# Gathering the tokens of two experts at once with float32r products

## The chip, the cores and the metric

The kernel runs on one core of one Trainium2 chip. The metric is device time in microseconds (us): the median of several executions. TensorE is called PE in the profile, VectorE DVE, ScalarE ACT, GpSimd POOL, and SyncE, whose queue issues the loads of weights, SP. PEld is TensorE's loading of the stationary operand, which overlaps its products.

## The reference, cut to what matters

Two transformer blocks for 256 tokens of 1024 features, all in float32. The change is in the last layer's mixture of experts: 8 experts, each token goes to two of them.

```python
def moe_swiglu(xn, router_w, w_gate_up, w_down):
    xf = xn.reshape(-1, d_)                                  # 256 tokens x 1024
    logits = (xf @ router_w).astype(jnp.float32)
    top_v, top_i = lax.top_k(logits, TOP_K)                  # 2 of 8
    top_w = jax.nn.softmax(top_v, axis=-1)
    combine = jnp.sum(jax.nn.one_hot(top_i, N_EXPERTS, dtype=jnp.float32) * top_w[..., None], axis=1)
    out = jnp.zeros_like(xf)
    for e in range(N_EXPERTS):
        out = out + combine[:, e:e + 1] * swiglu(xf, w_gate_up[e], w_down[e])   # silu(g) * u, 3584 wide
    return out.reshape(b_, s_, d_)
```

## The kernel before

Every large product is exact to float32 by three float32r products: a matrix x is split into hi (its float32r rounding, copied by ACT) and lo = x - hi (subtracted by DVE), and hi·hi, lo·hi and hi·lo are added up in PSUM. Activations are split once, weights as they stream in.

**The stream of weights.** `load` (L223) brings 1 MB with one DMA into one of 7 raw buffers, or, where the plan allows it ("ANY", the experts' weights and the last output product), with four DMAs of 256 KB into four pages of a pool of 50 pages of [128, 512]. `fill` (L359) issues loads as long as fewer than `room[0]` = 7 raw and fewer than `room[1]` paged loads are held; `room[1]` follows a table by stage (`ROOM_MOE`, `ROOM_ROUTED`, `ROOM_FIRST`, `ROOM`). All go through SP's queue in order. Each load is two pieces; `look_ahead` (L375) splits a piece three pieces ahead of its use: one ACT copy and one DVE subtraction of 1024 columns from a raw buffer, two of 512 columns each from pages.

**The order of the work** is the order in which the program is written, on each engine. `unit` (L452) is one slot: first the PE part of the next stage of a side generator, then the products with one piece of weights (six products of 512 columns in an expert), then the split of a later piece, deferred work, and the rest of the side's stage (evacuations on ACT and DVE). A side advances by two `yield`s per unit; sides put in front go first.

**An expert** (`expert`, L1507) is 7 gate/up steps `j` of 8 units, each followed by silu, multiplication and a transposition of the result (`at`, L1519; split into `ah`, `al`), and two column halves `n` of 14 units of the down product (`y`, L1560 to L1562), whose result is scattered back to the tokens by products with `selT` (`po`, L1570).

**The gather** (`prepare`, L1469) runs as a side of the previous expert's down product, one per expert. `sel` [token, slot] holds ones where a token has that place in the expert's list. Products of the tokens `xn` (float32, stationary) with `sel` (float32, 128 columns) give the expert's tokens, transposed, as `xe` in PSUM (L1488); ACT and DVE split them into `xeh` and `xel`. `sel` is then transposed into `selT` (L1501, L1503, L1505). For expert 0 the generator starts in `moe` (L1441 to L1447) right after the routing: two stages, the split of one more piece of weights, two stages more, and the rest as an "urgent" side of the first units. PSUM tiles of all sides (`sp`) share four buffers.

Of the kernel before, what the change touches and what calls it, by code (L numbers as in the profile page):

```python
# [31 lines left out]
# columns of the packed parameters  # L32
# [19 lines left out]
# columns of the constants that depend on shapes alone  # L52
# [5 lines left out]
def shape_constants():  # L58
# [16 lines left out]
    # masks of the decay levels: [s, level, t]; the first is the diagonal  # L75
# [5 lines left out]
    # one-hot buckets over the distance, [bucket, set, y]  # L81
    oh = np.zeros((33, 2, 384), np.float32)
    y = np.arange(384)
    dist = y - 127                     # query - key
# [18 lines left out]
# buffers: loads of weights (8 KB), pages (2 KB), pieces split ahead; first products for the clock  # L103
RAW_BUFS, PAGE_BUFS, LOOK, WARM = 7, 50, 3, 10
RAW, ANY = 1, 2          # a load goes into a raw buffer, or also into four pages
# loads that may be in pages: from the last layer's merge on; with the experts' start, after the routing;
# while the first expert runs (seven steps, two column halves); later
ROOM_MERGE, ROOM_MOE, ROOM_ROUTED, ROOM_FIRST, ROOM = 4, 5, 8, (8, 8, 7, 7, 6, 6, 6, 6, 6), 6


class Norm:
    """rmsnorm of the stream: the split stream times the gains (x), the root per token (rs, and as columns col)."""
# [4 lines left out]
    def then(self, f):  # L117
        """f needs the root."""
        if self.ready:
            f()  # L120
        else:
            self.waiting.append(f)


class Net:
    """The two blocks. Engines run in the order in which instructions are written here: between the
    products with one piece of the weights ("unit") and the next go the split of a later piece,
    the evacuation of the last result and a stage of the attention-like parts ("side")."""
# [59 lines left out]
    def rsqrt(self, out, ms, tmp, scale=None):  # L188
        """out = (scale * ms + eps) ** -0.5: by exp and log, and by what it returns, a step of Newton's method."""
# [26 lines left out]
    def warm(self, n, x):  # L216
        """products that nothing reads, for TensorE's clock to stay up while it has to wait"""
        ps = self.sp("warm")
        for _ in range(n):
            self.nc.tensor.matmul(ps, self.ones_r, x.rearrange("p a b -> p (a b)"), start=True, stop=True)  # L220

# [14 lines left out]
    # plans yield RAW or ANY before each load, and for each piece its view (or views) and how many loads it is the last one of  # L236
# [9 lines left out]
    @staticmethod  # L246
    def halves(v):
        """the two pieces of a load with all columns"""
        if isinstance(v, list):
            n = len(v) // 2  # L250
            return v[:n], v[n:]
        n = v.shape[1] // 2
        return v[:, :n, :], v[:, n:, :]
# [105 lines left out]
    def fill(self):  # L359
        """loads as far ahead as there are buffers."""  # L360
# [14 lines left out]
    def look_ahead(self, far=LOOK):  # L375
        """the split of a later piece: ScalarE's part now, VectorE's with the next call."""
# [46 lines left out]
    def defer(self, f, n=1):  # L423
        """f is to run n slots later, when the other engines are through with what it needs."""
        self.later.append((n, f))
# [15 lines left out]
    def stage(self, width):  # L441
        """the first half (TensorE) of the next stage of the first sides; what remains of them."""
# [25 lines left out]
    def drain(self, width=2, gens=None):  # L468
        """runs sides alone until those in gens (or all) are through."""
# [19 lines left out]
    def chunk_t(self, x, evac, kb=8, width=1):  # L489
        """[P, 2, T] in PSUM: 256 columns of the weights, transposed, times x; then evac."""  # L490
# [7 lines left out]
    def chunk_late(self, x, evac, width=1):  # L498
        """as chunk_t with 8 blocks, the last two of the contraction taken after the others of both halves."""
# [17 lines left out]
    def scaled(self, out, ps, N):  # L517
        """out [P, 2, T] = a product in PSUM (one page or two halves) times the root of the norm."""
# [6 lines left out]
    def chunk_tok(self, x, evac, width=1):  # L525
        """two [P, 256] in PSUM: tokens on partitions, 256 columns of the weights; then evac."""
# [14 lines left out]
    def chunk_tok_pair(self, x, evacs, width=1):  # L541
        """two chunks, the second halves of the contraction after both first ones."""
# [17 lines left out]
    def norm_feed(self, N, c):  # L560
        """chunk c of the stream is complete."""
        self.gain(N, c)
        self.squares(N, c, self.nc.gpsimd)
        if c == 3:
            self.first.append(self.norm_root(N))

    def gain(self, N, c):
        """chunk c of the stream times the gains, split."""
# [8 lines left out]
    def squares(self, N, c, e):  # L577
        """squares of chunk c, added up: those of the first three by the engine e, VectorE the rest."""
# [34 lines left out]
    def first_chunk(self, N, xr, evac):  # L613
        """the norm of the stream as it comes in, with the first 256 columns of the weights two blocks at a time."""
# [7 lines left out]
        # products of ones, for TensorE's clock to be up when the first data are there  # L622
# [39 lines left out]
    def bias_tiles(self, which):  # L662
        """stages that make [P, 2, 256] pages, one per two heads: the bias of queries 128.. over all keys."""
# [40 lines left out]
    def block1(self):  # L704
# [5 lines left out]
        # lower bound: softmax over the two rows of gamma, first row  # L710
# [89 lines left out]
        gates = [self.pgv(2, T, nm="gl") for _ in range(8)]      # per 128 columns: [P, branch, T]  # L800
# [33 lines left out]
    def residual(self, x, kb, g):  # L834
        """the stream plus the product; the norm that follows, with gain g."""
# [39 lines left out]
    def head_scale(self, pages, width, N=None):  # L875
        """stages: rmsnorm of pages [P(t), 2 (tile), 256] over each width channels, in place, gains apart;
        with N, of the pages times the root of that norm."""
# [37 lines left out]
    def flip(self, x):  # L915
        """a page [P(t), 2 (tile), 256 (head, d)] as [P(d), 2 (head), T] in PSUM."""
# [6 lines left out]
    def flip_heads(self, xs, gs):  # L923
        """stages: pages with heads, [P(d), 2 (head), T], times gains."""
# [10 lines left out]
    def hgrn(self, qs, fs, ks, vs, sgs, mk, c, o):  # L935
        """two heads: q, f, k [P(dk), 2, T]; v [P(s), 2 (tile), 256 (head, dv)]."""
# [7 lines left out]
        for lev in range(8):  # L944
# [14 lines left out]
            else:  # L959
                # block length w -> 2w  # L960
# [37 lines left out]
    def soft(self, ps, bias):  # L998
        """logits of the first 128 queries over 128 keys and of the last over 256, in PSUM:
        exp(logits + bias - max), and the sums."""  # L1000
# [4 lines left out]
        for t in (1, 0):       # the part that is written last first  # L1005
# [8 lines left out]
    def pv(self, pts, v, tokens):  # L1014
        """stages: pts are probabilities per head, tokens on partitions; their products with v in PSUM,
        [P(t), 2 (tile), 256 (head, dv)] if tokens, or [P(dv), 2 (head), T]."""
# [97 lines left out]
    def layer_setup(self, l):  # L1114
        """stages; small loads and what they are made into."""
# [20 lines left out]
        lam = S["nlam"] = c.tile([P, 1], F32, name=f"nlam{l}")      # minus lambda  # L1136
# [54 lines left out]
    def pool(self, pa, S, l, ya):  # L1191
# [8 lines left out]
        shift(s0, pa, 1, al, slice(0, 2))      # windows of 2  # L1200
        shift(s1, s0, 2, al, slice(0, 2))      # 4
        yield 1
        yield 1
        shift(s0, s1, 4, al, slice(1, 2))      # 8, block 1
        shift(s1, s0, 8, hi, slice(1, 2))      # 16
# [13 lines left out]
        for b in (1, 0):       # the part that is written last first  # L1219
# [20 lines left out]
    def mixer(self, l, N, S):  # L1240
# [45 lines left out]
        # gates: per 128 columns two pages [P, 2 branches, T]: (attention, pool), (conv, sgu)  # L1286
# [43 lines left out]
    def moe(self, merged):  # L1330
        """the last layer's output product, tokens on partitions; routing; the experts."""
# [11 lines left out]
        def evac(c, ps):  # L1343
            cs = slice(256 * c, 256 * c + 256)
            y = self.xn[c] = self.pgv(2, 256, nm="xn")
# [4 lines left out]
            def stages():  # L1350
# [9 lines left out]
                self.copy(z, pt)  # L1360
                yield 1
# [4 lines left out]
                yield 1  # L1366
                sq = self.pg(nm="sq")
# [14 lines left out]
        # logits before the root of the norm, which the order doesn't depend on  # L1382
# [3 lines left out]
        # rank of each expert: how many are larger, or equal with a lower index  # L1386
# [15 lines left out]
        # positions of the tokens in their experts' lists  # L1402
# [10 lines left out]
        def weights():  # L1413
            """the root of the norm, the weights (softmax over the two chosen) and the longest list"""
# [30 lines left out]
        for _ in range(2):  # L1445
# [12 lines left out]
    def overflow(self):  # L1458
        """experts with more than 128 tokens: all experts again, for the tokens from the 129th on."""
# [9 lines left out]
    def prepare(self, e, pos, ready):  # L1469
        """stages: the tokens at positions 0..127 of pos in expert e's list, gathered by products."""  # L1470
        nc = self.nc
        mm = nc.tensor.matmul
        sel, sT = self.pg(nm="sel"), self.pg(dt=F32R, nm="selT")
        xe = []
        ready[e] = xe, sT
        yield 1
        for t in range(2):
            nc.vector.tensor_scalar(sel[:, t * P:t * P + P], self.c[:, C_IOTA:C_IOTA + P], pos[:, 8 * t + e:8 * t + e + 1], None, op0=OP.is_equal)
# [4 lines left out]
        for half in range(2):  # L1483
            ps = self.sp("xe")
            for k in range(4):
                kk = 4 * half + k
# [212 lines left out]
```

## Time and profile before

| | |
|---|---|
| time, median of 3 runs | 2203.89 us (2203.86 to 2204.39) |
| profiled execution: span from first to last instruction | 2202.1 us |
| the page's own time for that execution | none given beside its span; the median run is 1.8 us above the span |
| PE busy | 2180.7 us, 99% |
| DVE busy | 1794.9 us, 82% |
| ACT busy | 1438.9 us, 65% |
| moved by DMA | 559.89 MB, mean 254 GB/s over the span |

The experts take roughly the last 1000 us of the span. In the page, a line such as `L1488 PE MATMUL xe<-sel,xn` names the source line, the engine, the operation and its output and inputs; a float32 product shows as two records, a float32r product as one. A PE record's duration includes the pipeline, so records overlap; how far PE moves on per record is read from the chain of work that ended last, whose pieces lie end to end.

### The profile page before, as it was taken

The page shows a single profiled execution, that of the slowest core. Times are in us where ns is not written, and L with a number is a line of the kernel's source. Part 1 is how long each engine was busy: PE and PEld are TensorE (multiplying, and loading weights), DVE is VectorE, ACT ScalarE, POOL GpSimd, SP SyncE. Part 2 cuts the span into 40 slices and gives each one's busy share as a digit, 9 for nine tenths or more (in the row PEclk, how much of TensorE's full clock was granted, in tenths as well). Part 3 has the DMA queues.
Part 4 walks back from the last instruction along what each step waited for, and adds up shares of the span by engine and source line. Part 5 has one row for each costly group of instructions (what it writes and reads, how often), then busy time and mean ns, then how long its engine had stood idle before and what let it go on. Part 6 is the DMA issues. An engine that isn't in the chain of part 4 may idle for free.

```text
span 2202.1 us, 38213 instructions
## 1 busy us (share of the span) xinstructions
PE 2180.7 (99%) x14473; PEld 2000.6 (91%) x14473; DVE 1794.9 (82%) x2669; ACT 1438.9 (65%) x2159; POOL 82.3 (4%) x89
## 2 busy tenths in 40 slices
PE   9999999999999999999999999999999999999998
PEld 9999999999999999999998888888888888888886
DVE  7876766655787966557877999999999999999997
ACT  6447555444555554455555878888787878888785
POOL 0000000003000300020020000000000000000000
PEclk9999999999999999999999999999999999999999
DMA  9434466547553655574458999999999999999992
GB/s 331 148 128 141 135 193 191 186 160 221 184 167 106 222 192 172 171 222 156 156 175 299 344 325 365 350 361 373 341 368 340 371 348 363 345 368 368 333 372 79
DMA packets 386369, 559.89 MB, mean 254 GB/s; under 512 B 17482, under 2 KB 212058, under 8 KB 386176
## 3 DMA queue, kind: packets, MB, share of 16 engines
q1 hardware_dynamic: 383792, 552.04, 72.7%
q0 software_dynamic: 2240, 5.28, 0.8%
q8 instruction: 115, 1.88, 0.4%
q14 instruction: 78, 0.64, 0.1%
q10 hardware_dynamic: 144, 0.05, 0.0%
HBM read 556.23 MB, written 1.07 MB: 253 GB/s over the span
## 4 chain that ended last, share of the span: by engine, by line
PE 96%; DVE 3%; DMA 1%; issue 0%; SPq 0%; ACT 0%; DVEq 0%
PE g L485 13%; PE g L487 12%; PE g L486 12%; PE g L1542 9%; PE g L1540 9%; PE g L1541 9%; PE y L1560 5%; PE y L1562 5%; PE y L1561 5%; PE g L537 3%; PE g L539 3%; PE g L538 3%; DVE lo L400 1%; PE xe L1488 1%; PE lev L950 1%; PE at L1519 1%
## 5 line engine op out<-in xcount | busy, mean ns | idle before, releaser
L183 ACT ACTIVATE hi<-raw 128x512 fp32r<-128x512 f32 (+1 forms) x1382 | 1137.5, 849 | 589.2 <-PE g L486 283.0
L400 DVE TENSOR_TENSOR lo<-raw,hi 128x512 fp32r<-128x512 f32 (+1 forms) x1378 | 1289.7, 971 | 183.7 <-ACT hi L183 158.1
L485 PE MATMUL g<-nh,hi 128*128 128x256 f32 x1696 | 485.7, 286 | 0.7 <-ACT hi L183 0.7
L487 PE MATMUL g<-nh,lo 128*128 128x256 f32 x1696 | 480.1, 283 | 1.2 <-DVE lo L400 0.8
L486 PE MATMUL g<-nl,hi 128*128 128x256 f32 x1696 | 479.7, 283 | 0.0
L1540 PE MATMUL g<-hi,xeh 128*128 128x512 f32 x896 | 353.2, 394 | 0.0
L1542 PE MATMUL g<-lo,xeh 128*128 128x512 f32 x896 | 349.6, 390 | 0.0
L1541 PE MATMUL g<-hi,xel 128*128 128x512 f32 x896 | 349.0, 389 | 0.0
L485 PEld LDWEIGHTS g<-nh,hi 128*128 128x128 f32 x1696 | 325.1, 192 | 4.4 <-issue 1.8
L487 PEld LDWEIGHTS g<-nh,lo 128*128 128x128 f32 x1696 | 325.1, 192 | 1.8 <-DVE lo L400 1.0
L486 PEld LDWEIGHTS g<-nl,hi 128*128 128x128 f32 x1696 | 325.3, 192 | 0.2
L1542 PEld LDWEIGHTS g<-lo,xeh 128*128 128x128 f32 x896 | 168.2, 188 | 36.1 <-DVE lo L400 0.8
L1541 PEld LDWEIGHTS g<-hi,xel 128*128 128x128 f32 x896 | 168.4, 188 | 33.6
L1540 PEld LDWEIGHTS g<-hi,xeh 128*128 128x128 f32 x896 | 168.3, 188 | 33.2
L1560 PE MATMUL y<-hi,ah 128*128 128x512 f32 x448 | 177.0, 395 | 0.0
L1562 PE MATMUL y<-lo,ah 128*128 128x512 f32 x448 | 174.6, 390 | 0.0
L1561 PE MATMUL y<-hi,al 128*128 128x512 f32 x448 | 174.4, 389 | 0.0
L537 PE MATMUL g<-hi,nh 128*128 128x256 f32 x480 | 139.2, 290 | 0.0
L539 PE MATMUL g<-lo,nh 128*128 128x256 f32 x480 | 135.7, 283 | 0.0
L538 PE MATMUL g<-hi,nl 128*128 128x256 f32 x480 | 135.7, 283 | 0.0
L1562 PEld LDWEIGHTS y<-lo,ah 128*128 128x128 f32 x448 | 84.1, 188 | 17.7
L485 PE MATMUL g<-ah,hi 128*128 128x256 f32 x352 | 99.6, 283 | 0.0
(384 smaller groups left out, 2955.4 us busy)
## 6 DMA issues: line engine op xcount, KB each, us to landing
raw<-in_moe_w_gate_up_dram SPq DMA_DIRECT2D x122, 1024.0 KB, 5.8
raw<-in_moe_w_gate_up_dram SPq DMA_DIRECT2D x408, 256.0 KB, 6.0
raw<-in_w_in_dram SPq DMA_DIRECT2D x90, 1024.0 KB, 5.2
raw<-in_moe_w_down_dram SPq DMA_DIRECT2D x60, 1024.0 KB, 5.7
raw<-in_moe_w_down_dram SPq DMA_DIRECT2D x208, 256.0 KB, 6.3
raw<-in_ffn_w_gate_up_dram SPq DMA_DIRECT2D x22, 1024.0 KB, 5.2
raw<-in_w_ffn_gate_dram SPq DMA_DIRECT2D x11, 1024.0 KB, 5.4
raw<-in_w_ffn_up_dram SPq DMA_DIRECT2D x11, 1024.0 KB, 5.5
```

Source lines behind the costliest of these rows:

```text
L183: return self.nc.scalar.activation(out, in_, func, **kw)
L400: self.nc.vector.tensor_sub(l, x, h)
L485: mm(out, hi[:, k, :], xh, start=r + k == 0, stop=False)
L486: mm(out, hi[:, k, :], xl, start=False, stop=False)
L487: mm(out, lo[:, k, :], xh, start=False, stop=r + k == kb - 1)
L537: mm(ps[t], xh[:, s], hi[:, k, :], start=r + k == 0, stop=False)
L1540: mm(ps, xh, hi[:, k, :], start=first, stop=False)
L1541: mm(ps, xl, hi[:, k, :], start=False, stop=False)
L1542: mm(ps, xh, lo[:, k, :], start=False, stop=last)
L1560: mm(py, xh, hi[:, i, :], start=k == 0, stop=False)
L1561: mm(py, xl, hi[:, i, :], start=False, stop=False)
L1562: mm(py, xh, lo[:, i, :], start=False, stop=k == KE - 1)
```

## The change

- The normalised tokens `xn` (float32) are split as they are made, in the last output product's evacuation: `xh` on ACT, `xl` on DVE, four pages each in place of four pages of `xn`.
- `prepare` runs for the experts e and e+1 together, as a side of the down product of experts 1, 3 and 5, and before expert 0. `sel` is now one float32r page with 256 columns per token half: 128 for each of the two experts. Per 256 features (`c`), the parts `xh` and `xl` are multiplied with it in float32r, in two PSUM tiles; the gathered parts need no subtraction: ACT copies the one tile to `hi`, DVE the other to `lo`. Each of the four rounds is a stage of its own.
- The transposition to `selT` is done for each of the two experts, in a stage of its own each.
- Before expert 0, four stages (two rounds) in place of two (one half) stand ahead of the first unit.
- Fewer paged loads may be held: the table goes from 8 after the routing and 6 in the steady state down to 6 and 2.

```diff
-ROOM_MERGE, ROOM_MOE, ROOM_ROUTED, ROOM_FIRST, ROOM = 4, 5, 8, (8, 8, 7, 7, 6, 6, 6, 6, 6), 6
+ROOM_MERGE, ROOM_MOE, ROOM_ROUTED, ROOM_FIRST, ROOM = 4, 5, 6, (6, 6, 5, 5, 4, 4, 3, 2, 2), 2
...
-            y = self.xn[c] = self.pgv(2, 256, nm="xn")
+            y = self.pgv(2, 256, nm="xn")
+            xh, xl = self.xn[c] = [self.pgv(2, 256, dt=F32R, nm="xn" + s) for s in "hl"]
...
                 self.copy(z, pt)
+                self.copy(xh, y)
...
+                nc.vector.tensor_sub(xl, y, xh)
                 sq = self.pg(nm="sq")
...
         self.split_next(LOOK + 1)
-        for _ in range(2):
+        for _ in range(4):
             next(prep)
...
-        sel, sT = self.pg(nm="sel"), self.pg(dt=F32R, nm="selT")
+        page = self.pg(dt=F32R, nm="sel")
+        sel = page.rearrange("p (t e s) -> p t e s", t=2, e=2)
         xe = []
-        ready[e] = xe, sT
+        sTs = [self.pg(dt=F32R, nm="selT") for _ in range(2)]
+        for i in range(2):
+            ready[e + i] = xe, i, sTs[i]
...
-        for half in range(2):
-            ps = self.sp("xe")
-            for k in range(4):
-                kk = 4 * half + k
-                for t in range(2):
-                    mm(ps[:, k * P:k * P + P], self.xn[kk // 2][:, t, (kk % 2) * P:(kk % 2) * P + P], sel[:, t * P:t * P + P], start=t == 0, stop=t == 1)
-            yield 1
-            hi, lo = self.pg(dt=F32R, nm="xeh"), self.pg(dt=F32R, nm="xel")
-            self.copy(hi, ps)
-            sub = lambda ps=ps, hi=hi, lo=lo: nc.vector.tensor_sub(lo, ps, hi)
-            self.defer(sub) if e else sub()
-            xe.append((hi, lo))
+        for c in range(4):
+            pages = []
+            for x in self.xn[c]:
+                ps = self.sp("xe")
+                for k in range(2):
+                    for t in range(2):
+                        mm(ps[:, 256 * k:256 * k + 256], x[:, t, k * P:k * P + P], page[:, 256 * t:256 * t + 256], start=t == 0, stop=t == 1)
+                pages.append((ps, self.pg(dt=F32R, nm="xe")))
+            yield 1
+            (ph, hi), (pl, lo) = pages
+            self.copy(hi, ph)
+            nc.vector.tensor_copy(lo, pl)
+            xe.append([v.rearrange("p (k e s) -> p k e s", k=2, e=2) for v in (hi, lo)])
             yield 1
...
-            if n == 0 and e + 1 < NE:
+            if n == 0 and e % 2 and e + 1 < NE:
                 self.side(self.prepare(e + 1, pos, ready))
```

How PE's row stands where the tokens of expert 2 are gathered, in the down product of expert 1 (`y`: the down product, `xe`: the gathered tokens in PSUM, `x4`: four products). Before:

```order
L1488 MATMUL xe_16612<-sel_16553,xn_14116 128x128 x4
L1488 MATMUL xe_16612<-sel_16553,xn_14153 128x128 x4
L1560 MATMUL y_16552<-hi_16579,ah_16137 128x512
L1561 MATMUL y_16552<-hi_16579,al_16138 128x512
L1562 MATMUL y_16552<-lo_16588,ah_16137 128x512
L1488 MATMUL xe_16635<-sel_16553,xn_14241 128x128 x4
L1488 MATMUL xe_16635<-sel_16553,xn_14295 128x128 x4
```

Now, for experts 2 and 3 together:

```order
L1497 MATMUL xe_16492<-sel_16430,xnh_14117 128x256 x4
L1497 MATMUL xe_16498<-sel_16430,xnl_14118 128x256 x4
L1571 MATMUL y_16429<-hi_16459,ah_16034 128x512
L1572 MATMUL y_16429<-hi_16459,al_16035 128x512
L1573 MATMUL y_16429<-lo_16468,ah_16034 128x512
L1497 MATMUL xe_16517<-sel_16430,xnh_14156 128x256 x4
L1497 MATMUL xe_16523<-sel_16430,xnl_14157 128x256 x4
L1571 MATMUL y_16429<-hi_16470,ah_16034 128x512
```

The three rows of `y` stand twice between two groups in both programs and are shown once. Two groups of eight float32 products per expert have become four groups of eight float32r products per pair, each ahead of one piece's products.

DVE's row at the start of the experts (`sel`: the ones and zeros; L400: the subtraction of a piece of weights; `xel`, then `xe`: the low part of the gathered tokens). Before:

```order
L1478 TENSOR_SCALAR sel_14386<-consts,pos 128x128 x2
L400 TENSOR_TENSOR lo_14390<-raw_13655,hi_14288 128x1024
L400 TENSOR_TENSOR lo_14394<-raw_13655,hi_14392 128x1024
L1492 TENSOR_TENSOR xel_14408<-xe_14398,xeh_14407 128x512
L1492 TENSOR_TENSOR xel_14431<-xe_14412,xeh_14430 128x512
L1422 TENSOR_REDUCE sm_14443<-ss_13956 128x2
```

Now:

```order
L1486 TENSOR_SCALAR sel_14386<-consts,pos 128x128 x4
L400 TENSOR_TENSOR lo_14393<-raw_13655,hi_14297 128x1024
L400 TENSOR_TENSOR lo_14397<-raw_13655,hi_14395 128x1024
L1502 CAST xe_14412<-xe_14407 128x512
L1502 CAST xe_14426<-xe_14421 128x512
L1502 CAST xe_14441<-xe_14436 128x512
L1502 CAST xe_14464<-xe_14459 128x512
```

The two subtractions of weights still stand between `sel` and the first evacuation of gathered tokens. On PE, three of the four rounds (24 products) now stand ahead of the first product with weights, and the fourth ahead of the second piece; the two float32 halves all stood ahead of the first. Of the 336 loads of the experts' weights, 80 are now paged, 154 before.

More of the change, by code (lines that the diff above doesn't have):

```diff
@@ L1472, in prepare @@
         mm = nc.tensor.matmul
-        sel, sT = self.pg(nm="sel"), self.pg(dt=F32R, nm="selT")
+        page = self.pg(dt=F32R, nm="sel")
+        sel = page.rearrange("p (t e s) -> p t e s", t=2, e=2)
         xe = []
-        ready[e] = xe, sT
+        sTs = [self.pg(dt=F32R, nm="selT") for _ in range(2)]
+        for i in range(2):
+            ready[e + i] = xe, i, sTs[i]
         yield 1
         for t in range(2):
-            nc.vector.tensor_scalar(sel[:, t * P:t * P + P], self.c[:, C_IOTA:C_IOTA + P], pos[:, 8 * t + e:8 * t + e + 1], None, op0=OP.is_equal)
+            for i in range(2):
+                nc.vector.tensor_scalar(sel[:, t, i, :], self.c[:, C_IOTA:C_IOTA + P], pos[:, 8 * t + e + i:8 * t + e + i + 1], None, op0=OP.is_equal)
         if e:
@@ L1498, in prepare @@
                 yield 1
-        ps = self.sp("selT")
-        for t in range(2):
-            nc.tensor.transpose(ps[:, t * P:t * P + P], sel[:, t * P:t * P + P], self.ident)
-        for t in range(2):
-            mm(ps[:, T:T + 1], sel[:, t * P:t * P + P], self.rs[:, t:t + 1], start=t == 0, stop=t == 1)
-        yield 1
-        nc.vector.tensor_copy(sT[:, :T + 1], ps[:, :T + 1])
+        for i in range(2):
+            sT = sTs[i]
+            ps = self.sp("selT")
+            for t in range(2):
+                nc.tensor.transpose(ps[:, t * P:t * P + P], sel[:, t, i, :].bitcast(F32), self.ident)
+            for t in range(2):
+                mm(ps[:, T:T + 1], sel[:, t, i, :].bitcast(F32), self.rs[:, t:t + 1], start=t == 0, stop=t == 1)
+            yield 1
+            nc.vector.tensor_copy(sT[:, :T + 1], ps[:, :T + 1])
+            yield 1
     def expert(self, e, pos, ready):
@@ L1509, in expert @@
         mm = nc.tensor.matmul
-        xe, sT = ready.pop(e)
+        xe, own, sT = ready.pop(e)
         rs = sT[:, T:T + 1].bitcast(F32)
@@ L1536, in gu_products @@
             for k in range(2):
-                kk = 2 * q + k
-                first, last = r + kk == 0, r == 1 and kk == 3
-                xh, xl = (xe[r][i][:, kk * P:kk * P + P] for i in range(2))
+                first, last = r + q + k == 0, r + q + k == 3
+                xh, xl = (v[:, k, own, :] for v in xe[2 * r + q])
                 mm(ps, xh, hi[:, k, :], start=first, stop=False)
```

## The prediction

> **What bounds the kernel now.** I read the page's busy shares and its chain first, then windows over whole experts, then the chain around one gather, and last the rows of the work that the change adds.
>
> ```profile
> PE 2180.7 (99%) x14473; PEld 2000.6 (91%) x14473; DVE 1794.9 (82%) x2669; ACT 1438.9 (65%) x2159; POOL 82.3 (4%) x89
> PE 96%; DVE 3%; DMA 1%; issue 0%; SPq 0%; ACT 0%; DVEq 0%
> L1542 PE MATMUL g<-lo,xeh 128*128 128x512 f32 x896 | 349.6, 390 | 0.0
> ```
>
> PE is busy all the time, 96% of the chain lies on it, and the product that waits for the last thing made of a piece of weights (its low part) never sat idle in 896 instances. Four experts, each from one gather to the next:
>
> ```profile
> core 0: us, PE busy (x) PEld busy (x) DVE busy (x) ACT busy (x) POOL busy (x), PEclk, DMA share, GB/s
> 1290.90:1414.60 123.70, 123.70 (x581) 103.09 (x580) 116.52 (x146) 100.99 (x139) 0.00 (x0) 1.00 0.99 355
> 1414.60:1538.30 123.70, 123.70 (x580) 103.06 (x579) 116.33 (x149) 101.17 (x142) 0.00 (x0) 1.00 1.00 357
> 1328.40:1408.30 79.90, 79.90 (x365) 66.19 (x365) 77.31 (x96) 67.64 (x93) 0.00 (x0) 1.00 1.01 368
> 1575.80:1655.70 79.90, 79.90 (x365) 66.18 (x364) 77.09 (x101) 67.95 (x97) 0.00 (x0) 1.00 1.02 370
> ```
>
> An expert takes 123.7 us, PE is full, its granted clock is 1.00. DVE follows at 116.4 of 123.7 us (94%), ACT at 101. The DMA engines are at a share of 1.0 too, with 355 to 357 GB/s over an expert and 368 to 370 over the gate/up part (last two rows). So a microsecond taken from PE comes off the time, provided DVE and the stream of weights can go a little faster than now.
>
> **The gather before.** In the chain around one gather the pieces lie end to end, so they show how far PE moves on:
>
> ```profile
> 1290.51 0.23 PE y L1562
> 1290.74 1.78 PE xe L1488 x16
> 1292.53 0.23 PE y L1560
> ...
> 1293.68 0.23 PE y L1562
> 1293.90 1.78 PE xe L1488 x16
> 1295.69 0.23 PE y L1560
> ...
> 1297.07 0.22 PE selT L1501 x2
> 1297.28 0.34 PE selT L1503 x4
> 1297.62 0.34 PE y L1560
> ```
>
> One half of the features costs 1.78 us, eight float32 products of two records each, 0.111 us a record; an expert costs 3.57 us. The transposition to selT costs 0.22 + 0.34, and 0.11 more on the product behind it, 0.67 us. Expert 0 shows the same 3.57, at the start of the experts:
>
> ```profile
> 1191.94 0.12 PE g L537
> ...
> 1195.51 0.94 PE warm L220 x4
> 1196.45 0.81 PE rt L1365 x8
> 1197.26 2.43 PE warm L220 x10
> ...
> 1199.91 1.03 PE warm L220 x4
> 1200.94 3.57 PE xe L1488 x32
> ```
>
> Eight experts make 8 x 3.57 = 28.6 us on PE, all on the path.
>
> **The gather after.** A pair has four rounds of eight float32r products, 128 x 128 stationary and 256 columns moving: 32 products. The nearest row has this shape and type: the output product's L537 moves PE on by 0.12 us (first row of the last fence). That is 3.84 us a pair, 15.4 us for four. The transpositions stay eight groups of 0.67 us: nothing. The difference is 28.6 - 15.4 = 13.2 us.
>
> By the Trainium skill ("TensorE: Matmul & The Clock Gate", Back-to-back issue gap), a product of N columns takes N / 2.4 + 2.5 ns when warm, which is 109 ns for 256 columns; an estimate from that page's formula makes the gain 1.4 us larger. The trace does not agree: 120 ns here for 256 columns, so I keep the row.
>
> Bounds of this term: at most 0.12 us per product plus a change-over like selT's 0.11 us per round (16 rounds, 1.8 us less gain); at least 0.111 us, the float32 record's step (1.2 us more). I take 0.12, since shape and type are the same.
>
> **The start.** Four ones-and-zeros pages' writes stand where two stood, and two subtractions of weights stand between them and the evacuations:
>
> ```profile
> 1200.16 0.48 DVE L1478 TENSOR_SCALAR sel<-consts,pos 128x128 f32<-128x128 f32 x2
> 1200.56 2.35 DVE L400 TENSOR_TENSOR lo<-raw,hi 128x1024 fp32r<-128x1024 f32 x2
> 1203.39 0.69 DVE L1492 TENSOR_TENSOR xel<-xe,xeh 128x512 fp32r<-128x512 f32 x1 [0.48 <-ACT xeh L183]
> ```
>
> Two writes are 0.4 us apart from what follows, four 0.8: ready near 1201.0, the dummy products run to 1200.94, so PE loses about 0.1. Two rounds, 1.92 us, end near 1202.9. The third round needs PSUM buffers of the first (four buffers, two a round): its high part is out early, but its low part's DVE copy starts behind the subtractions, at 1203.3, and ends at 1204.0. PE, done with the third round's high half at 1203.4, waits 0.6 us. Loss at the start 0.6 to 0.7 us; from 0, if the write order lets PE begin on the first half, to 1.3, if both parts of the next round wait for a 0.69 us copy. I take 0.7.
>
> Ahead of it, the splits of xn are four ACT copies and four subtractions in the routing's run-up. Three lie beside the output product. The last subtraction stands ahead of the logits on DVE and makes these some 0.3 us late; the ten dummy products (2.43 us, to 1199.68) end after the routing's ranks are due, and take it up. Without that cover it would be 0.3 us.
>
> **Work off the path.** These rows give its prices:
>
> ```profile
> L400 DVE TENSOR_TENSOR lo<-raw,hi 128x1024 fp32r<-128x1024 f32 x698 | 848.8, 1227 | 156.6 <-ACT hi L183 135.5
> L400 DVE TENSOR_TENSOR lo<-raw,hi 128x512 fp32r<-128x512 f32 x648 | 414.5, 696 | 9.8 <-ACT hi L183 5.2 <-PE b L486 1.2
> L1616 DVE COPY acc<-ht x4: 683/692/692, 971.1 to 980.2; 128x512 f32<-128x512 f32 x4
> L183 ACT ACTIVATE xeh<-xe x16: 597/597/598, 1202.8 to 2037.9; 128x512 fp32r<-128x512 f32 x16
> L183 ACT ACTIVATE hi<-raw 128x1024 fp32r<-128x1024 f32 x698 | 736.4, 1059 | 480.4 <-PE g L486 245.9 <-PE g L538 86.8 <-PE g L1541 52.2
> raw<-in_moe_w_gate_up_dram SPq DMA_DIRECT2D x408, 256.0 KB, 6.0
> DMA to landing us min/median/max: 3.3/5.5/14.3
> SPq L229 <- DMA raw<-in_moe_w_gate_up_dram: 107.8, 174, 3.2
> ```
>
> DVE: a pair had four subtractions `xel` of 0.69 us (last fence but one), and has four copies out of PSUM, nearest row L1616, 0.69 us: no change. A paged load costs DVE 4 x 0.696 against 2 x 1.227 us for a raw one, 0.33 us more; 74 fewer of them take 24 us off DVE over the experts, 3 us each. DVE then needs 113.4 of 122 us. In a gather's unit PE needs 0.96 + 6 x 0.23 = 2.34 us, DVE 1.23 + 0.69 = 1.92 (2.08 with a paged piece), ACT 1.06 + 0.60 = 1.66: both are through before PE, and the two PSUM buffers of a round are wanted again two units later. So the evacuations cost nothing; without that cover each would cost up to 0.69 us.
>
> Loads: an expert has 336 / 8 = 42 loads of 1.049 MB, one per 123.7 / 42 = 2.95 us. Held loads fall from 7 + 6 to 7 + 2, 38 us ahead to 26.5 us ahead, some 4 us of it taken by the splits. The raw loads land after 5.5 us in the median and 14.3 us at worst (row with the three landing times), so each still lies 8 us or more in its buffer before its split: nothing. What would be late next, if it were not so, is ACT's copy of a piece. The stream has to bring 44.0 MB in 123.7 - 13.2 / 8 = 122.05 us, 361 GB/s; the windows show 368 to 370 over 79.9 us: nothing.
>
> **The sum.** -28.6 + 15.4 + 0.7 = -12.5 us: on the profiled execution's span 2202.1 - 12.5 = 2189.6 us. The median run is 1.8 us above that span, which the change doesn't touch: 2203.9 - 12.5 = 2191.4 us. Its own range goes from 1.2 us more gain with no loss at the start (2189.5) to 1.8 us less gain and 1.3 us of loss (2193.8).
>
> **The rivals.**
>
> *The evacuations stop PE in the middle gathers.* For it: DVE is 94% busy, does its work in a fixed order, and the low copy stands behind a piece's subtraction; four PSUM buffers now turn over every second unit and are shared with the transposed activations. Against it: 1.92 against 2.34 us. If each of the 12 rounds behind the first four waits for half a copy to a whole one, 0.35 to 0.69 us, 4 to 8 us go: 2195.6 to 2199.7, middle 2197.6.
>
> *The stream becomes the bound.* For it: the DMA share is 1.0 through whole experts. Against it: 368 to 370 GB/s for 80 us, with PE never waiting. If 357 GB/s were all it can keep up, an expert would take 44.0 / 0.357 = 123.3 us, the gain would be 8 x 0.4 = 3 us, and the time 2200.7, within 0.2%.
>
> The Trainium skill ("DMA: Bandwidth & Descriptors", the table at its head) names about 358 GB/s as a core's limit from HBM. By it an estimate is 44.0 / 0.358 = 123.0 us an expert, 5.6 us of gain and 2198.3 us, and less gain lost as long as buffered loads last. The trace doesn't agree for this core alone: 368 to 370 GB/s.
>
> *The products don't get cheaper.* If a float32r product of these operands took the two records of a float32 one, a product would cost 0.22 us, 128 of them 28.4 us, and the time would be 2204.4 with the start's loss: no change. Against it: all of the kernel's float32r products of this shape show one record and 0.12 us.
>
> *Slower: a paged load stops the queue.* SP issues in order. While a pair is prepared its sel, selT and xe pages (11) stand beside the split tokens (8), the transposed activations (14) and the held loads (8) in 50 pages. A paged load that waits there for a page holds back all raw loads behind it. PE stops once a hold lasts longer than 26.5 - 4 - 5.5 = 17 us, and at three gathers the gain is gone with 17 + 12.5 / 3 = 21 us each. A hold for a whole column half with its gather (14 x 1.36 + 3.84 + 1.34 = 24 us) would cost 7 x 3 = 21 us: 2212.4. Against it: the paged loads' longest wait is 3.2 us (last row above), and the change cuts the number of them.
>
> **How the numbers follow.** The forecast has 0.78, the evacuations 0.10, the stream 0.05, products that don't get cheaper 0.02, the stopped queue 0.05. 0.2% is 4.4 us, about what a measurement of this kernel can tell from no change: faster is below 2199.5, slower above 2208.3. So faster 0.88, same 0.07, slower 0.05. The range 2189.0 to 2197.6 holds the forecast and the cheaper half of the evacuations' case.
>
> **What would show it.** Right: 128 records of gather products at 128x256 in one form, chain pieces of about 0.96 us for eight of them, four of them per pair in the down products of experts 1, 3 and 5 and none in those of 0, 2, 4 and 6; expert 0 starts with a small PE wait for DVE's copy; a stretch from one pair's gather to the next of about 244 us where two experts took 247.4; no PE wait for `lo` or `hi`. Wrong: PE idle before a gather product, released by a DVE copy, in the middle gathers (first rival); ACT's copies waiting for DMA, with landings over 10 us and a rate that stays at 357 GB/s (second); two records per gather product (third); a wait of SP of many microseconds at a paged load (fourth).

## The result, and the profile after

The changed kernel takes 2189.99 us (median of 5 runs, 2188.27 to 2190.23) against 2203.86 us before (5 runs, 2203.66 to 2204.39): a ratio of 0.9935, 95% interval 0.9923 to 0.9947. The forecast was 2191.4. The profiled execution has a span of 2186.5 us and took 2188.27, again 1.8 us more. It is the fastest of the five: the median run took 1.7 us longer.

The page after: busy shares, the chain's shares, and the product that takes the low part of a piece.

```profile
PE 2167.7 (99%) x14345; PEld 1987.7 (91%) x14345; DVE 1790.5 (82%) x2525; ACT 1426.9 (65%) x2015; POOL 82.3 (4%) x89
PE 95%; DVE 2%; DMA 2%; issue 0%; SPq 0%; ACT 0%; DVEq 0%
L1553 PE MATMUL g<-lo,xe 128*128 128x512 f32 x896 | 349.9, 390 | 0.2 <-DVE lo L400 0.2
```

PE has lost 13.0 us of busy time and still bounds the kernel; the low part was late once in 896 times, by 0.2 us, at expert 0.

The gather's products and their evacuations (instructions of the tile `xe`, with shortest, median and longest duration in ns):

```profile
L1497 PE MATMUL xe<-sel,xnh x64: 277/283/386, 1200.5 to 1906.8; 128*128 128x256 f32 x64
L1497 PE MATMUL xe<-sel,xnl x64: 278/283/284, 1201.3 to 1907.3; 128*128 128x256 f32 x64
L1502 DVE CAST xe<-xe x16: 680/692/696, 1203.0 to 1907.6; 128x512 fp32r<-128x512 f32 x16
```

One record for each of the 128 products. Two gathers in the chain, of the pair prepared under expert 1 and of the next pair, under expert 3 (start, length, what):

```profile
1411.38 0.95 PE xe L1497 x8
1413.72 0.95 PE xe L1497 x8
1416.06 0.95 PE xe L1497 x8
1418.39 0.95 PE xe L1497 x8
1420.74 0.22 PE selT L1512 x2
1420.96 0.34 PE selT L1514 x4
...
1655.45 0.95 PE xe L1497 x8
```

Each round moves PE on by 0.95 us, four rounds a pair, and from one pair to the next it is 1655.45 - 1411.38 = 244.07 us, where two experts took 247.4.

To compare kernels apart from how a run starts and ends, I take the main part, from the first product of the tile `rc`, 26 us into the span, to the start of the last down product `y`, and the end, from PE's last product to the span's end. The rows that mark the main part, of before (two rows) and after:

```profile
L608 PE MATMUL rc<-ones,rs x20: 245/245/266, 26.5 to 969.4; 1*128 1x1 f32 x20
L1562 PE MATMUL y<-lo,ah x448: 388/389/398, 1285.1 to 2189.8; 128*128 128x512 f32 x150
```

```profile
L608 PE MATMUL rc<-ones,rs x20: 245/246/267, 26.2 to 969.2; 1*128 1x1 f32 x20
L1573 PE MATMUL y<-lo,ah x448: 388/390/398, 1286.4 to 2176.8; 128*128 128x512 f32 x150
```

With the records' times to two decimals, as in all rows of this table:

| kernel | median us | main part us | end us |
|---|---|---|---|
| before | 2203.86 | 2163.22 | 9.55 |
| after | 2189.99 | 2150.59 | 6.93 |
| e1, table alone | 2202.02 | 2163.24 | 7.55 |
| e2, pair in float32 | 2202.04 | 2162.97 | 7.94 |
| e3, float32r, one expert per product | 2202.14 | 2163.31 | 7.58 |
| e4, products twice | 2204.60 | 2165.71 | 7.69 |
| e5, before with loads that never run | 2202.40 | 2163.24 | 7.25 |
| e6, after with loads that never run | 2189.52 | 2150.41 | 8.00 |
| e7, selT in float32r | 2187.42 | 2148.87 | 8.06 |
| e8, five loads ahead | 2189.23 | 2150.38 | 7.87 |
| e9, e7 with later weights | 2187.78 | 2148.90 | 7.84 |

The main part gives 12.63 us. The medians differ by 13.87, so 1.2 us come from somewhere else; the kernel before stands out with its end. The ends in the table are those of the profiled executions. The main part repeats to about 0.2 us: e6 and e8 do the same products in it as the changed kernel, in 0.18 and 0.21 us less.

### The profile page after: what moved, and what is told of

Read it like the earlier page. It is cut to its first block, busy times and chain, and to the rows that moved or that the text cites. A ratio compares the mean times of both kernels' runs of the same rounds, so it can differ in the third digit from the quotient of the medians.

```text
span 2186.5 us, 37140 instructions
## 1 busy us (share of the span) xinstructions
PE 2167.7 (99%) x14345; PEld 1987.7 (91%) x14345; DVE 1790.5 (82%) x2525; ACT 1426.9 (65%) x2015; POOL 82.3 (4%) x89
## 4 chain that ended last, share of the span: by engine, by line
PE 95%; DVE 2%; DMA 2%; issue 0%; SPq 0%; ACT 0%; DVEq 0%
PE g L485 13%; PE g L486 13%; PE g L487 13%; PE g L1553 9%; PE g L1551 9%; PE g L1552 9%; PE y L1571 5%; PE y L1573 5%; PE y L1572 5%; PE g L537 3%; PE g L539 3%; PE g L538 3%; PE lev L950 1%; PE at L1531 1%; DVE lo L400 1%; PE xe L1497 1%
## 5 line engine op out<-in xcount | busy, mean ns | idle before, releaser
L183 ACT ACTIVATE hi<-raw 128x1024 fp32r<-128x1024 f32 (+1 forms) x1234 | 1125.0, 928 | 603.0 <-PE g L486 283.0
L400 DVE TENSOR_TENSOR lo<-raw,hi 128x1024 fp32r<-128x1024 f32 (+2 forms) x1230 | 1283.9, 1071 | 184.0 <-ACT hi L183 148.1
L1551 PE MATMUL g<-hi,xe 128*128 128x512 f32 x896 | 353.6, 395 | 0.0
L1553 PE MATMUL g<-lo,xe 128*128 128x512 f32 x896 | 349.9, 390 | 0.2 <-DVE lo L400 0.2
L1552 PE MATMUL g<-hi,xe 128*128 128x512 f32 x896 | 349.3, 390 | 0.0
L1553 PEld LDWEIGHTS g<-lo,xe 128*128 128x128 f32 x896 | 168.2, 188 | 35.8 <-DVE lo L400 0.6
L1552 PEld LDWEIGHTS g<-hi,xe 128*128 128x128 f32 x896 | 168.5, 188 | 33.5
L1551 PEld LDWEIGHTS g<-hi,xe 128*128 128x128 f32 x896 | 168.4, 188 | 33.2
L486 PE MATMUL g<-al,hi 128*128 128x256 f32 x352 | 99.8, 283 | 0.0
```

Source lines behind the costliest of these rows:

```text
L183: return self.nc.scalar.activation(out, in_, func, **kw)
L400: self.nc.vector.tensor_sub(l, x, h)
L486: mm(out, hi[:, k, :], xl, start=False, stop=False)
L1551: mm(ps, xh, hi[:, k, :], start=first, stop=False)
L1552: mm(ps, xl, hi[:, k, :], start=False, stop=False)
L1553: mm(ps, xh, lo[:, k, :], start=False, stop=last)
```

## The experiments

The kernel before took 2204.28 us beside e1 to e4, 2204.15 beside e5 to e8 and 2204.08 beside e9.

**e1: the table alone.**

```diff
 (in the kernel before)
-ROOM_MERGE, ROOM_MOE, ROOM_ROUTED, ROOM_FIRST, ROOM = 4, 5, 8, (8, 8, 7, 7, 6, 6, 6, 6, 6), 6
+ROOM_MERGE, ROOM_MOE, ROOM_ROUTED, ROOM_FIRST, ROOM = 4, 5, 6, (6, 6, 5, 5, 4, 4, 3, 2, 2), 2
```

> The kernel before with the change's table of held paged loads (6 after the routing, 2 in the steady state) and nothing else. Theory (the loads' lead was cover that nobody needed, and DVE is off the path): paged loads fall from 154 to about 80, and the time stays at 2203.9 us within 1 us. Rival A (part of the gain came from the cheaper splits of raw loads, some 3 us of DVE work per expert): 2198 to 2202. Rival B (the shorter lead costs something that the gather's gain hid): above 2206.

2202.02 us, ratio 0.9991 (0.9982 to 1.0000). The main part is that of before to 0.02 us: fewer paged loads neither help nor hurt the experts. The 2 us lie in the end, 7.55 against 9.55 us; e5 takes that up. So the time left my theory's 1 us and fell into rival A's range, but not for rival A's reason, which would have shown in the main part.

**e2: the pair at once, but in float32.** One 256-column float32 product in place of two float32r ones, then copy and subtraction as before.

```diff
 (in the changed kernel)
+            self.xn[c] = y                      # float32, not split
...
+            ps = self.sp("xe")
+            for k in range(2):
+                for t in range(2):
+                    mm(ps[:, 256 * k:256 * k + 256], x[:, t, k * P:k * P + P], page[:, 256 * t:256 * t + 256], start=t == 0, stop=t == 1)
...
+            self.copy(hi, ps)
+            sub = lambda ps=ps, hi=hi, lo=lo: nc.vector.tensor_sub(lo, ps, hi)
+            self.defer(sub) if e else sub()
```

> The change with float32 operands in the gather: two experts at once, 256 columns, but no split of xn, 16 float32 products a pair, and copy plus subtraction behind them. Theory (float32r is what saves): a float32 record of 256 columns moves PE on by about 0.217 us, two records a product, 16 x 0.434 = 6.9 us a pair plus 4 x 0.11 for the change-overs, 29 us in all: 2203 to 2205 us. Rival (taking two experts at once is what saves, since the records get fewer): 0.111 us a record, 14 us in all, 2189 to 2191.

**e3: float32r, but one expert's 128 columns per product.**

```diff
 (in the changed kernel)
-                    for t in range(2):
-                        mm(ps[:, 256 * k:256 * k + 256], x[:, t, k * P:k * P + P], page[:, 256 * t:256 * t + 256], ...)
+                    for i in range(2):
+                        for t in range(2):
+                            mm(ps[:, 256 * k + P * i:256 * k + P * i + P], x[:, t, k * P:k * P + P], page[:, 256 * t + P * i:256 * t + P * i + P], ...)
```

> The change with each gather product cut in two of 128 columns, one per expert: 256 float32r products in place of 128, all else the same. Theory (a float32r product costs its columns at 2.4 per ns and 13 ns more, from 120 ns at 256 columns and 227 ns at 512): 67 ns each, 17.1 us in place of 15.4, 2191.7 us. Rival A (narrow float32r products fall back to a float32 product's time, 222 ns): 56.8 us, about 2231. Rival B (each product is held to its weight load, some 107 ns): 27.4 us, about 2202.

e2 took 2202.04 us (ratio 0.9989, 0.9980 to 0.9998), e3 2202.14 (0.9991, 0.9981 to 1.0000). In the chain a round under expert 1 reads, first in e2 and then in e3:

```profile
1418.26 1.73 PE xe L1494 x8
```

```profile
1417.70 1.73 PE xe L1498 x16
```

A float32 record with 256 columns moves PE on by 1.73 / 8 = 0.216 us, a float32r product with 128 columns by 1.73 / 16 = 0.108, as a float32 record with 128 did (0.111). So neither half of the change is worth anything alone: the main parts are 2162.97 and 2163.31 against 2163.22 us. In e2 my theory held: the pair costs what the single experts cost, and the time lies under the forecast by the shorter end, as in e1. In e3 the outcome was rival B's and my theory was wrong: a 128-column product does not get cheaper in float32r.

What the step of 0.108 us consists of can be read in e3's trace. The chain from the start of the same round, up to its first and up to its second product:

```profile
1417.70 0.06 PE xe L1498
1417.70 0.17 PE xe L1498 x2
```

By the start times of the records, the second product of a round begins 57 to 60 ns after the first, in all rounds but the first three; every later one begins 111 ns after the one before it, and the loads of weights (PEld) begin 112 ns apart (medians). The router's float32 records `rt`, with only 8 columns moving, do the same: 30 to 45 ns to the second, 112 ns from then on. So the moving columns do not set this step; each of these records has a weight load of its own, and in e3 the products follow at the loads' pace. The Trainium skill ("TensorE: Matmul & The Clock Gate", LDWEIGHTS) puts a weight load at its columns / 1.2 ns, an estimate of 107 ns for 128, which agrees. With 256 columns, a step of 0.12 us then pays one load for two experts. That the load is the limit in e3 is read from these start times; no run took the load away.

**e4: every gather product twice.**

```diff
 (in the changed kernel)
-                    for t in range(2):
+                    for t in (0, 1, 0, 1):
```

> The change with each gather product done twice (the second time overwrites the first). Theory (the products are on the path at 0.12 us each and nothing else in the gather is): 128 x 0.12 = 15.4 us more, 2205.4 us. Rival (evacuations or waits around a round set its time, and PE has room): less than 10 us more, below 2200.

2204.60 us, main part 15.12 us over the changed kernel's (expected 15.4). A round of 16 took 1.91 us:

```profile
1419.01 1.91 PE xe L1497 x16
```

So 0.119 us a product holds with the work doubled, and all of it is on the path; from 1195 to 2185 us PE waits once, for the 0.2 us at expert 0. Doubled, the gather costs as much as before: 2204.60 us is about the 2204.4 that rival three had as its price. That rival itself is refuted by one record per product.

**e5 and e6: loads that never run.** Twenty loads are written into the branch for over-long experts, which isn't entered; e5 is the kernel before, e6 the changed one.

```diff
             self.act_set = None
+            for i in range(20):
+                nc.sync.dma_start(self.pg(nm="never"), self.a["moe_w_gate_up_2"][0, 0, 0:P, 512 * (i % 7):512 * (i % 7) + 512])
             pos = self.sm(16, nm="pos2")
```

> The kernel before, with 20 loads written into the branch for over-long experts, which is never entered: no instruction more is executed, SP's instructions for what follows only lie at other addresses. It asks where the about 2 us come from that the new table alone took off the end of the program (from TensorE's last product to the span's end 9.55 us in the kernel before, 7.55 us with the new table, 6.93 us in the changed kernel). Theory: SP waits there for its own instruction fetch (SP stood 2.1 us between two of its waits, with a fetch of 8 KB in it), which depends on where its instructions lie; moved by 20 loads, the end takes about 7.5 us and the kernel 2202, with the main part (start of the routing to the last product) at 2163.2 us as before. Rival: the end is shorter because of the loads themselves (fewer outstanding transfers, other queue state); then this kernel stays at 2204 with an end of 9.5 us. A third outcome, an end of 7.5 us in some runs only, would make it chance.

> The changed kernel with the same 20 loads in the branch that is never entered. Main part as in the changed kernel, 2150.6 us, by every theory. If the end depends on where SP's instructions lie, it is either 7 us (2190) or 9 us (2192) here; if it depends on the loads, 7 us and 2190. It is also a second measurement of the changed kernel's gain on another chip: 12.6 us of the main part.

e5 took 2202.40 us, 1.75 us less than the kernel before (ratio 0.9992, 0.9983 to 1.0001), with an end of 7.25 us. The interval just reaches 1, but the slowest of its 11 runs (2203.49) is under the fastest of the 15 runs beside it of the kernel before (2203.52). e6 took 2189.52 (0.9935, 0.9922 to 0.9949), the changed kernel's gain again: between e5 and e6 the medians differ by 12.88 us and the main parts by 12.83. Waits of SP's queue from 2170 us to the end (in total, times, longest), in before, in e5 and in after:

```profile
SPq L1462 <- SPq L1462: 4.8, 2, 2.7
```

```profile
SPq L1462 <- SPq L1462: 2.6, 1, 2.6
```

```profile
SPq L1465 <- SPq L1465: 2.7, 1, 2.7
```

L1462 and L1465 are the branch at the program's end. SP's instructions there take signals one after the other; in the kernel before, two of them lie 2.1 us apart (2197.97 to 2200.08), and one 8 KB packet of the instruction queue was taken in that gap, at 2198.60. Where instructions only lie at other addresses, the second wait is gone. The loads that run are the same in both, so the 1.8 us at the end belong to the program's layout, not to the loads. That SP waited for that very packet is the likely reading, but only its time speaks for it. All nine experiments, laid out otherwise, have ends of 7.25 to 8.06 us, and the changed kernel has 6.93: the kernel before had the bad layout.

e6's end of 8.00 us met neither of its two forecasts, 7 or 9. SP's issuing of the last two stores of the output, in after and in e6, has the difference:

```profile
2179.91 1.02 SPq L1588 DMA_DIRECT2D out_dram<-acc  x2
```

```profile
2179.58 2.01 SPq L1590 DMA_DIRECT2D out_dram<-acc  x2
```

The second of these issues took 0.36 us in the changed kernel's profiled execution and 0.81 to 1.39 us in all ten others. What makes it longer stays open; it is why the changed kernel's 6.93 us is the shortest end of all.

**e7: selT in float32r too.** Two products per expert, `sel` stationary, moving 130 columns (the identity and the two float32r parts of the root), in place of two transpositions and two one-column float32 products.

```diff
 (in the changed kernel)
             for t in range(2):
-                nc.tensor.transpose(ps[:, t * P:t * P + P], sel[:, t, i, :].bitcast(F32), self.ident)
-            for t in range(2):
-                mm(ps[:, T:T + 1], sel[:, t, i, :].bitcast(F32), self.rs[:, t:t + 1], start=t == 0, stop=t == 1)
+                mm(ps[:, (P + 2) * t:(P + 2) * (t + 1)], sel[:, t, i, :], self.spread[t], start=True, stop=True)
...
+            nc.vector.tensor_reduce(self.root[e + i], both[:, :, P:P + 2], axis=AX.XY, op=OP.add)
```

> The changed kernel, with the transposed selection and the experts' roots also made by float32r products: two per expert, the selection stationary, 130 columns moving (the identity and the root's two parts), in place of two float32 transposes and two one-column float32 products (0.67 us per expert in the changed kernel's trace). Theory: the step of a 128-column float32r product was 0.111 us, so 0.22 us per expert, 0.45 us less, 8 times: 3.6 us off, 2186.4 us, beating both kernels; VectorE does two small operations more per expert beside TensorE. Rival: the selections' products are hidden in nothing but the first pair's stands at the start behind VectorE's chain, and the product reads a copy that VectorE makes there 0.2 us later, so only 3 us come; or VectorE, 82% busy, gives some of it back: 2188 or more.

2187.42 us, ratio 0.9924 (0.9911 to 0.9938): 2.1 us faster than e6 beside it, and faster than both kernels. But the main part is 1.72 us under the changed kernel's, not 3.6. Under the experts the theory holds: the down product with a preparation fell from 44.80 to 43.89 us, 0.45 an expert. At the start it does not. PE's waits from 1195 to 2185 us, in after and in e7:

```profile
PE po L1581 <- ACT yh L183: 0.7, 1, 0.7
PE po L1582 <- DVE yl L1593: 0.2, 1, 0.2
PE g L1553 <- DVE lo L400: 0.2, 1, 0.2
```

```profile
PE g L1557 <- DVE lo L400: 1.1, 1, 1.1
PE po L1585 <- ACT yh L183: 0.7, 1, 0.7
PE po L1586 <- DVE yl L1597: 0.2, 1, 0.2
```

At expert 0 the low part of a piece comes 1.1 us late instead of 0.2: PE is there earlier, and four small DVE operations that split the root (0.6 us) stand ahead of it. The steps of the gate/up part also got 0.08 us longer per expert (79.91 to 79.99 us), some 0.6 us in all, which I did not explain.

**e8: five loads ahead instead of nine.**

```diff
 (in the changed kernel)
-            self.room[1] = ROOM if e else ROOM_FIRST[j]
+            self.room = [5, ROOM] if e else [7, ROOM_FIRST[j]]      # and ROOM = 0; the same in the down product
```

> The changed kernel with only five loads held ahead instead of nine from the second expert on (no paged loads there at all). Of the changed kernel's loads the slack from landing to first use was about 16 us with nine held; each load feeds about 2.9 us of products, so four fewer leave about 4 us. Theory: the stream still comes in time, no wait of TensorE, 2190 as the changed kernel, and fewer paged loads cost nothing. Rival (a lead this short is too little when a transfer lands late): TensorE waits at some splits, the step of a load goes from 2.9 us towards the time of a load's issue and landing over five held, and the time goes over 2195.

2189.23 us (0.9933, 0.9918 to 0.9948), main part 2150.38. From a load's landing to its split it was about 10 us (8.0 at least, experts 2 to 7; by the records of all loads), against 16 in the changed kernel and 28 before: the slack fell less than the 12 us I had reckoned, and PE never waited for it:

```profile
PE po L1581 <- ACT yh L183: 0.7, 1, 0.7
PE po L1582 <- DVE yl L1593: 0.2, 1, 0.2
PE g L1553 <- DVE lo L400: 0.2, 1, 0.2
```

**e9: e7 with the combine weights' last steps later.**

```diff
 (in e7, in weights(): the count's maximum moved up, then)
+            for _ in range(16):
+                yield 1
             nc.vector.tensor_mul(comb, comb, ind.bitcast(F32))
```

> The kernel of e7 with VectorE's last operations on the combine weights (four small ones: product, sum, reciprocal, product; 0.8 us) moved back by 16 pieces of the first expert, whose weights are first needed about 100 us later. In e7 TensorE waited 1.13 us at the first expert for the low half of a piece of weights, since VectorE reached it only after the chain of small operations. Theory: that wait is VectorE's lateness, so it shrinks by about 0.8 us to 0.3, TensorE waits nowhere else, and the kernel comes to 2186.6. Rival: VectorE is late at the start whatever it does last (it is near full from there on), and the four operations only move the wait to a later piece: 2187.4 as e7.

2187.78 us (0.9924, 0.9910 to 0.9937), main part 2148.90, as e7. The wait moved, as the rival had it, but for another reason. DVE and then ACT of e9 at expert 0:

```profile
1210.56 1.21 DVE L400 TENSOR_TENSOR lo<-raw,hi 128x1024 fp32r<-128x1024 f32 x1
1213.03 2.36 DVE L400 TENSOR_TENSOR lo<-raw,hi 128x1024 fp32r<-128x1024 f32 x2 [1.26 <-ACT hi L183]
```

```profile
1210.41 0.21 ACT L183 ACTIVATE comb<-comb 128x16 f32<-128x16 f32 x1 [1.96 <-DVE comb L1436]
1210.64 1.28 ACT L178 ACT_TABLE_LOAD   x1
1211.94 2.01 ACT L183 ACTIVATE hi<-raw 128x1024 fp32r<-128x1024 f32 x2
```

DVE is early now and stands idle for 1.26 us: it waits for the high part, which ACT makes only after the exponential (for which ACT itself waited 1.96 us on DVE's chain) and a table load of 1.28 us. PE waits 0.5 us for the next low part and 0.2 us elsewhere. By these rows, what sets the start is the chain root, logits, exponential, table, next split; moving the exponential, or the root's split behind it, could shorten it. That was not tried.

## Why the prediction was right, step by step

**The gather** was right: 8 records in 0.95 us against the 0.96 forecast, 4 x 4 of them, no change-over between rounds, and everything on the path (e4). Main part -12.63 us against the sum's -12.5. The nearest row, the output product's with the same shape and type, was the right one to take; e2 and e3 show that the float32 record and the 128-column product would each have given no gain. The 109 ns that the formula of the Trainium skill ("TensorE: Matmul & The Clock Gate", Back-to-back issue gap) gives for 256 columns are not reached: 119 ns. The Trainium skill calls that formula there the gap of an isolated product, and says that in a stream the weight load counts too.

**The start** came out near its size, but by luck: half of its mechanism did not happen. I had 0.1 us for the two more writes of `sel` and 0.6 us for a wait of the third round on DVE's copy. The chain and DVE's copies show:

```profile
1200.70 0.14 PE xe L1497
1200.85 3.01 PE xe L1497 x23
1203.86 0.13 PE cnt L1419
```

```profile
1202.98 1.88 DVE L1502 CAST xe<-xe 128x512 fp32r<-128x512 f32 x3
1203.22 0.64 PE L1497 MATMUL xe<-sel,xnl 128*128 128x256 f32 x4
```

The 24 products of three rounds take 3.16 us where 24 x 0.12 = 2.88 would do: 0.28 us for `sel`'s writes, more than forecast. But the third round's low half (last row, PE) starts at 1203.22, before DVE's first copy can have ended at 1202.98 + 0.69: its PSUM buffer was not the one that this copy reads, and nothing waited. Instead PE lost 0.2 us at the low part of a later piece, since the fourth copy (0.69 us) and the weights' chain stand ahead of it on DVE. Some 0.5 us together, against 0.7. The main part says the same: of the 13.2 us without a loss, 12.6 came (12.8 in e6 and e8). The "small PE wait for DVE's copy" among the signs was wrong, and so was the sign that PE would never wait for a `lo`.

**The stream and the queue** were right: the shorter lead costs nothing (e1 main part, e8 with even less), the share of the DMA engines stays full at a higher rate, and no paged load held up SP for long. SP's longest kind of wait at a paged load (in total, times, longest), and a window of one pair:

```profile
SPq L229 <- DMA raw<-in_moe_w_gate_up_dram: 59.4, 50, 2.4
```

```profile
core 0: us, PE busy (x) PEld busy (x) DVE busy (x) ACT busy (x) POOL busy (x), PEclk, DMA share, GB/s
1352.00:1596.09 244.09, 244.09 (x1126) 202.92 (x1125) 230.77 (x256) 198.49 (x241) 0.00 (x0) 1.00 1.01 362
```

At a paged load the queue waits 2.4 us at most. Before, the longest wait there was 3.8 us and not the 3.2 that I took: my row held only the waits for landings, and one for a page that the products of `selT` still read was longer:

```profile
SPq L229 <- PE selT L1503: 5.2, 2, 3.8
```

362 GB/s over 244 us is above the 357 of the second rival; it had been 355 to 357 only because PE asked for no more. It is also above the 358 GB/s that the Trainium skill names ("DMA: Bandwidth & Descriptors", the table at its head); the Trainium skill works it out there as half of what two cores share, and this kernel runs on one core.

**DVE's relief was over-sized**, without effect. I gave each paged load 0.33 us more than a raw one and 24 us in all, from durations that overlap. The subtractions from 1200 to 2190 us, by form, of before and of after (busy us behind the bar):

```profile
L400 DVE TENSOR_TENSOR lo<-raw,hi 128x1024 fp32r<-128x1024 f32 x362 | 436.4, 1223 | 37.1 <-ACT hi L183 16.4
L400 DVE TENSOR_TENSOR lo<-raw,hi 128x512 fp32r<-128x512 f32 x616 | 386.4, 685 | 5.8 <-ACT hi L183 2.5
```

```profile
L400 DVE TENSOR_TENSOR lo<-raw,hi 128x1024 fp32r<-128x1024 f32 x510 | 615.5, 1223 | 41.7 <-ACT hi L183 8.4
L400 DVE TENSOR_TENSOR lo<-raw,hi 128x512 fp32r<-128x512 f32 x320 | 200.3, 687 | 1.2 <-ACT hi L183 0.3
```

822.8 us became 815.8: 7 us for 74 paged loads, 0.1 us each. DVE stays at 115.4 us an expert, not 113.4, and still under PE's 122.

**What lies around the span** is where the sum failed: I took the end as unchanged. The kernel before loses about 1.8 us at its end to the place of SP's instructions (e5), and the change, by writing fewer loads, moved these (e1). Of the 1.4 us by which the time came out under the forecast, the main part has 0.1 and what lies outside it 1.2; with both kernels laid out anew (e5 against e6), the medians differ by 12.88 us, hardly more than the main parts. So about 1 us of the 1.4 is layout, which no term of the sum stood for. The first rival, evacuations that stop PE, did not occur in any round.

## What to carry to other kernels

When a stationary operand is multiplied with few columns, look at how far PE moves on per product at the next larger width: here 128 and 256 columns cost 0.108 and 0.119 us in float32r, so joining two users of the same stationary operand nearly halves the cost, while a cheaper number format alone gave nothing here at 128 columns. Take steps from the chain, where pieces lie end to end, rather than from durations, which overlap on DVE too. When a change of 0.1% counts, compare the main part between two marks, and test with instructions that never run whether a gain comes from the program's layout.

## What the runs showed of the hardware that was not expected

Twenty instructions on SP that are never executed made a program 1.75 us faster, by taking away a 2.1 us gap in SP's last instructions. And a 128-column product in float32r takes as long as a record of a float32 product with 128 columns (0.108 and 0.111 us), while with 256 columns the two stand at 0.119 and 0.216 us. In e3 the second product of a round begins only 57 to 60 ns after the first: the rest of the 0.11 us is not the columns', and the weight loads have the same pace.
